# The output products of a feed-forward by seven block products in place of eight, with transferred low parts and moved conditioning rows

## The chip, the cores and the metric

The kernel runs on one core of a Trainium2 chip. The metric is the time of one execution on the device in microseconds, lower is better. The engines are TensorE (PE in the profile, its weight loads PEld), VectorE (DVE), ScalarE (ACT), GpSimd (POOL) and SyncE (SP, which issues most DMAs).

## The reference: what is computed

One decoder block on 512 tokens of width 1024, in fp32. Nine modulation vectors of 1024 come from the condition `c`; each of three sub-layers is normalised, scaled and shifted by them, and its result is added with a gate. The first and the last sub-layer are feed-forwards of hidden width 2816 (22 tiles of 128), at half weight:

```python
def swiglu(u, w_in, w_out):
    a, b = jnp.split(u @ w_in, 2, axis=-1)
    return (jax.nn.silu(a) * b) @ w_out
```

Between them stands the mixer: a pooling branch and a dilated attention with rotary queries and keys, both multiplied by sigmoid gates, summed and projected. A last RMSNorm gives the output.

## The kernel before

**High and low parts.** Every fp32 matrix product is made of three products of shorter numbers. An operand is split into a high part and a low part (what is left), and `mm3` or `product` sums high by high, high by low and low by high (lines 357 to 359; 739 to 741; 865 to 867). Weights come by DMA from HBM, 512 KB a chunk (128x1024), into raw buffers (SP's queue, line 235). ACT copies the high part into `whi` (line 312), DVE subtracts to get `wlo` (line 326). Both lie in a ring of seven chunks, and the splits run four products ahead of the one that TensorE works on (`look(4)`).

**Seven products for eight.** Where two hidden tiles of both halves are made together (`duo`), the product of 2x2 blocks is made by seven block products with sums before and behind (the scheme of Strassen and Winograd). A block product is 24 matmuls of 256 columns. The sums of activations come from `u_steps` (high copy at line 705, low part at 706; tiles `S0` to `S2`), the sums of weights from `make` on DVE (line 251, tiles X), and the results are put together by ACT copies out of the PSUM banks (line 746) and DVE adds. `out_quad` does the same for an output: four hidden tiles times eight output tiles, seven products, with its own sums of hidden tiles in `h_sums` (line 831 is ACT's copy, 828 the add). With `outer`, the low part of some of the seven weight chunks is made without DVE: ACT writes the negative high part into `wlo` (line 308), and an accumulating DMA of GpSimd's queue adds the weight from HBM (line 310).

**The feed-forwards.** `ffn` goes through five parts of hidden tiles, `PARTS` = (0..4, 4..8, 8..12, 12..16, 16..22). In each it makes the hidden tiles, with those of the next part's first duo, then multiplies the part by the output weights and adds to the state H. In the first feed-forward the tiles up to 7 are made singly (`ffn_pair`), the rest by duos, all low parts by DVE, and the outputs of all parts plainly: 96 matmuls of 512 columns for four parts (loop at line 970, H updated at line 985). In the second feed-forward the tiles up to 3 are single; the four first outputs go through `out_quad`, and two of every seven low parts (the fourth and the sixth chunk, counted from 0 numbers 3 and 5) come by transfer, in its duos from the second one on and in its block outputs.

**Conditioning rows.** The modulation vectors take 72 rows of 512 KB (`wada`), one DVE multiply with a running sum each (line 380). In the first feed-forward `bg()` does rows 24 to 47, beside the single tiles 6 and 7 and then one per output tile, from two buffers (`cs`, `AR`); the next row is fetched when a buffer is free. Rows 48 to 71 come in the mixer's end.

**The mixer.** It is written out in one order by hand; `mm_tile` takes hooks that run after a given block of a tile. Four value tiles (v23) precede the gates; `at_merge` (lines 1231 to 1248, DVE) combines the attention groups, `at_yT` transposes the result on TensorE (line 1255), and the low parts of the pooled branch (PL) stand at line 1290.

**Queues.** Each engine works its instructions in the order in which the program issues them; `later(n, f)` puts f behind the n-th product from now.

## Time and profile before

| | us |
|---|---|
| median of 3 runs | 1012.51 (1011.1 to 1012.77) |
| profiled execution | 1010.66 |
| its span | 1008.8 |
| plain output, parts 1 to 3 of the first feed-forward | 21.78 to 21.79 |
| block output, second feed-forward | 19.04 to 19.27 |

The granted clock of the profiled execution is 0.996 of full speed on average. A row of the timeline gives start, duration, engine, line, output and inputs, and in brackets how long the engine stood idle before it and what released it. A row of a group gives its count, its busy time and mean duration, then the idle time before it.

### The profile page before, as it was taken

The numbers are of one execution on the slowest core, as the hardware profiler recorded it, in microseconds if no ns is written. First come the engines' busy times: TensorE is split into PE (matmuls) and PEld (weight loads), VectorE is DVE, ScalarE is ACT, GpSimd is POOL, SyncE is SP. The second block draws the span as 40 slices with busy tenths as digits, with TensorE's granted clock in tenths as the row PEclk, the third lists the DMA queues.
The fourth block names the chain that finished last, engine by engine and source line by source line (L and its number), as shares of the span: only waits on it lengthen the run. The fifth ranks groups of instructions, "written<-read, shape, count | busy, mean of one in ns | idle before, by whom it ended". The sixth has DMA issues, their size and how long they took to land.

```text
span 1008.8 us, 16370 instructions
## 1 busy us (share of the span) xinstructions
PE 994.6 (99%) x6652; PEld 913.9 (91%) x6652; DVE 788.6 (78%) x1182; ACT 496.4 (49%) x754; POOL 47.3 (5%) x54
## 2 busy tenths in 40 slices
PE   8999999999999999999999999999899999999997
PEld 6888898989999999889988888898899999999996
DVE  7978879889787676879447777567998988989754
ACT  6443253625434552233414333463677768677652
POOL 0000000000000000007100000000011011011001
PEclk9999999999999999999999999999999999999998
DMA  9866456555533413122054774322467666756712
GB/s 341 275 224 228 140 195 189 175 164 185 168 99 117 145 46 99 58 84 84 32 185 161 272 261 134 92 78 63 146 147 178 177 147 155 201 130 164 178 32 84
DMA packets 46574, 152.24 MB, mean 151 GB/s; under 512 B 5281, under 2 KB 8609, under 8 KB 46498
## 3 DMA queue, kind: packets, MB, share of 16 engines
q1 hardware_dynamic: 42354, 137.95, 41.3%
q0 software_dynamic: 3456, 12.58, 7.5%
q8 instruction: 52, 0.85, 0.3%
q10 hardware_dynamic: 688, 0.66, 0.2%
q14 instruction: 24, 0.20, 0.1%
HBM read 148.40 MB, written 2.77 MB: 150 GB/s over the span
## 4 chain that ended last, share of the span: by engine, by line
PE 90%; DVE 7%; ACT 1%; issue 1%; DMA 0%; DVEq 0%; ACTq 0%
PE bank L357 14%; PE bank L358 14%; PE bank L359 14%; PE bank L739 10%; PE bank L741 9%; PE bank L740 9%; PE bank L867 3%; PE bank L866 3%; PE bank L865 3%; DVE wlo L326 1%; PE bank L1616 1%; PE bank L1620 1%; PE bank L1618 1%; PE bank L1212 1%; PE bank L1391 1%; PE bank L1392 1%
## 5 line engine op out<-in xcount | busy, mean ns | idle before, releaser
L326 DVE TENSOR_TENSOR wlo<-raw,whi 128x1024 fp32r<-128x1024 f32 (+7 forms) x157 | 156.7, 1011 | 56.0 <-ACT whi L312 55.8
L312 ACT ACTIVATE whi<-raw 128x1024 fp32r<-128x1024 f32 (+7 forms) x172 | 150.6, 894 | 31.2 <-DVE raw L251 27.6
L357 PE MATMUL bank<-UH,whi 128*128 128x512 f32 (+1 forms) x432 | 158.0, 366 | 0.0
L358 PE MATMUL bank<-UL,whi 128*128 128x512 f32 (+1 forms) x432 | 154.0, 357 | 0.1
L359 PE MATMUL bank<-UH,wlo 128*128 128x512 f32 (+1 forms) x432 | 153.9, 356 | 0.0
L741 PE MATMUL bank<-UH,wlo 128*128 128x256 f32 x512 | 141.6, 277 | 0.0
L739 PE MATMUL bank<-UH,whi 128*128 128x256 f32 x512 | 141.5, 276 | 0.0
L740 PE MATMUL bank<-UL,whi 128*128 128x256 f32 x512 | 141.5, 276 | 0.0
L326 DVE TENSOR_TENSOR wlo<-X,whi 128x1024 fp32r<-128x1024 f32 (+4 forms) x102 | 111.4, 1099 | 30.8 <-ACT whi L312 30.5
L312 ACT ACTIVATE whi<-X 128x1024 fp32r<-128x1024 f32 (+4 forms) x111 | 105.6, 966 | 40.6 <-DVE X L251 39.6
L739 PE MATMUL bank<-SH,whi 128*128 128x256 f32 x384 | 108.0, 281 | 3.0 <-ACT u L746 2.2
L740 PE MATMUL bank<-SL,whi 128*128 128x256 f32 x384 | 107.6, 280 | 0.0
L741 PE MATMUL bank<-SH,wlo 128*128 128x256 f32 x384 | 107.5, 280 | 0.0
L357 PE MATMUL bank<-HI,whi 128*128 128x512 f32 (+1 forms) x278 | 96.8, 348 | 0.0
L358 PE MATMUL bank<-HK,whi 128*128 128x512 f32 (+1 forms) x278 | 96.5, 347 | 0.0
L740 PEld LDWEIGHTS bank<-UL,whi 128*128 128x128 f32 x512 | 96.2, 188 | 0.2
L359 PE MATMUL bank<-HI,wlo 128*128 128x512 f32 (+1 forms) x278 | 96.4, 347 | 0.0
L741 PEld LDWEIGHTS bank<-UH,wlo 128*128 128x128 f32 x512 | 96.1, 188 | 0.2 <-DMA wlo<-wf2i 0.2
L739 PEld LDWEIGHTS bank<-UH,whi 128*128 128x128 f32 x512 | 96.1, 188 | 0.2
L359 PEld LDWEIGHTS bank<-UH,wlo 128*128 128x128 f32 x432 | 81.1, 188 | 12.1
L358 PEld LDWEIGHTS bank<-UL,whi 128*128 128x128 f32 x432 | 81.2, 188 | 11.7 <-issue 0.5
L357 PEld LDWEIGHTS bank<-UH,whi 128*128 128x128 f32 x432 | 81.2, 188 | 11.2 <-issue 0.5
(300 smaller groups left out, 2104.1 us busy)
## 6 DMA issues: line engine op xcount, KB each, us to landing
ada<-wada SPq DMA_DIRECT2D x47, 512.0 KB, 5.3
raw<-wmix SPq DMA_DIRECT2D x44, 512.0 KB, 4.1
raw<-wf1i SPq DMA_DIRECT2D x34, 512.0 KB, 4.5
raw<-wf2i SPq DMA_DIRECT2D x30, 512.0 KB, 3.7
wlo<-wf2i POOLq DMA_DIRECT2D x16, 512.0 KB, 6.3
X<-wf2i SPq DMA_DIRECT2D x14, 512.0 KB, 4.3
cs<-wada SPq DMA_DIRECT2D x12, 512.0 KB, 3.7
AR<-wada SPq DMA_DIRECT2D x12, 512.0 KB, 4.4
```

The lines of the kernel that those rows point to most:

```text
L312: self.nc.scalar.activation(self.hi[:, y], r[:, x], AF.Copy)
L326: self.nc.vector.tensor_tensor(self.lo[:, y], r[:, x], self.hi[:, y], op=OP.subtract)
L357: M(ps, hi, uh, start=start, stop=False)
L358: M(ps, hi, ul, start=False, stop=False)
L359: M(ps, lo, uh, start=False, stop=stop)
L739: M(o, hi, uh, start=start and p == 0 and k == 0, stop=False, skip_group_check=True)
L740: M(o, hi, ul, start=False, stop=False, skip_group_check=True)
L741: M(o, lo, uh, start=False, stop=k == 3, skip_group_check=True)
L865: M(o, hi, uh, start=start and m % 2 == 0 and k == 0, stop=False, skip_group_check=True)
L866: M(o, hi, ul, start=False, stop=False, skip_group_check=True)
L867: M(o, lo, uh, start=False, stop=k == 1, skip_group_check=True)
L1212: M(o, pt[:, blk * P:blk * P + P], v, start=i == 0, stop=i == len(srcs) - 1)
```

## The change

- The outputs of parts 1 to 3 (tiles 4 to 15) of the first feed-forward go through `out_quad`; its hidden sums and evictions come with it. Part 0 and the last part stay plain.
- In the first feed-forward's duos of tiles 10 to 21 and in its three block outputs, three of seven low parts (chunks 0, 3 and 5) come by transfer.
- The conditioning rows 24 to 39 are done in the first feed-forward, 24 to 27 with the single tiles 6 and 7, then two per duo (`beside`, after its third and sixth product). Rows 40 to 47 go to the mixer, into the one buffer `AR`, with one row fetched at a time.
- Buffers: the ring of hidden tiles has 4 places in the first feed-forward (`nh`), with three tiles `kept` of its own; the block outputs collect their results in `kept`; some high and low copies of hidden tiles come later (8 products behind a duo of the even kind, halves of tiles 4 and 5 after 5 and 6 products).
- Second feed-forward: `u_steps` puts a sum between each high copy and its low part, the low parts of tiles 0 to 3 are put off, and the hidden sums of part 0 start two products later.

Where it moves instructions (rows of the programs' order, without times; names with numbers are tiles). DVE in the mixer, around the start of the merge (`mm` is the merge's first operation, raw_66 and the like are weight buffers). Before:

```order
L326 TENSOR_TENSOR wlo<-raw_67,whi 128x1024
L1216 COPY q_3191<-bank_104 128x256
L326 TENSOR_TENSOR wlo<-raw_68,whi 128x512
L1290 SCALAR_TENSOR_TENSOR PL_3173<-bank_104,vecs,PH_3171 128x512
L1290 SCALAR_TENSOR_TENSOR PL_3174<-bank_98,vecs,PH_3172 128x512
L326 TENSOR_TENSOR wlo<-raw_66,whi 128x1024
L1231 TENSOR_TENSOR mm<-m_3200,v_3197 128x16
```

After:

```order
L1244 COPY q_3517<-bank_104 128x256
L381 SCALAR_TENSOR_TENSOR AR,mod<-AR,cond 128x1024
L327 TENSOR_TENSOR wlo<-raw_68,whi 128x512
L1318 SCALAR_TENSOR_TENSOR PL_3499<-bank_104,vecs,PH_3497 128x512
L1318 SCALAR_TENSOR_TENSOR PL_3500<-bank_102,vecs,PH_3498 128x512
L381 SCALAR_TENSOR_TENSOR AR,mod<-AR,cond 128x1024
L327 TENSOR_TENSOR wlo<-raw_66,whi 128x1024
L381 SCALAR_TENSOR_TENSOR AR,mod<-AR,cond 128x1024
L1259 TENSOR_TENSOR mm<-m_3526,v_3523 128x16
```

Three conditioning rows (44, 45 and 46, line 381 now) stand among the rows ahead of the merge, the last one directly before it.

DVE at the start of the second feed-forward (line 664, now 670, makes a hidden tile, 667 or 678 its low part HK; 699 or 725 are sums of activations, 706 or 733 the low part SL of one). Before:

```order
L664 TENSOR_TENSOR cond<-sl,bank_98 128x512
L667 TENSOR_TENSOR HK<-cond,HI 128x512
L715 TENSOR_TENSOR X<-UH,UL 128x1024 x2
L664 TENSOR_TENSOR cond<-p_5891,bank_100 128x512
L667 TENSOR_TENSOR HK<-cond,HI 128x512
L699 TENSOR_TENSOR X<-X 128x1024
L706 TENSOR_TENSOR SL_5609<-X,SH_5608 128x1024
L699 TENSOR_TENSOR X<-X 128x1024
```

After:

```order
L670 TENSOR_TENSOR cond<-sl,bank_98 128x512
L741 TENSOR_TENSOR X<-UH,UL 128x1024
L678 TENSOR_TENSOR HK<-cond,HI 128x512
L741 TENSOR_TENSOR X<-UH,UL 128x1024
L670 TENSOR_TENSOR cond<-u_6225,bank_100 128x512
L725 TENSOR_TENSOR X<-X 128x1024
L678 TENSOR_TENSOR HK<-cond,HI 128x512
L725 TENSOR_TENSOR X<-X 128x1024
L733 TENSOR_TENSOR SL_5951<-X,SH_5950 128x1024
```

Between a tile and its low part there now stands another sum.

ACT in the first feed-forward's output of part 1, from the first duo ahead of it (`sl` of the silu) on. Before:

```order
L769 ACTIVATE sl<-bank_97 128x2x256
L312 ACTIVATE whi<-X 128x256
L312 ACTIVATE whi<-X 128x768
L312 ACTIVATE whi<-X 128x1024
L746 ACTIVATE HI<-hf 128x1024
L312 ACTIVATE whi<-X 128x1024
L312 ACTIVATE whi<-raw_68 128x1024
```

After:

```order
L791 ACTIVATE sl<-bank_101 128x2x256
L313 ACTIVATE whi<-X 128x1024
L868 ACTIVATE bank_97<-bank_98 128x512
L868 ACTIVATE bank_102<-bank_99 128x512
L309 ACTIVATE wlo<-X 128x1024
L313 ACTIVATE whi<-X 128x1024
L868 ACTIVATE sl<-bank_100 128x512
L868 ACTIVATE sl<-bank_101 128x512
L313 ACTIVATE whi<-X 128x1024
L868 ACTIVATE kept_123<-bank_98 128x2x256
```

The copies out of the banks (line 868 now) and the negative copies for the transfers (line 309) stand among the high parts of the weights (line 313).

The diff, cut to its core:

```diff
-        def blocks(recs, outer=False):
+        def blocks(recs, outer=0):
             n = len(self.loads)
             if outer:
                 self.outer.update({len(self.order) + 3: n + 3, len(self.order) + 5: n + 2})
+            if outer == 3:
+                self.outer[len(self.order)] = n
...
                     else:
-                        blocks(ins[at:at + 4], n == 2 and j > PLAIN[n])
...
                         j, at = j + 2, at + 4
-                put = blocks if n and part < len(PARTS) - 1 else plain
+                put = blocks if (n or part) and part < len(PARTS) - 1 else plain
                 put(outs[part * KT // 2:(part + 1) * KT // 2] if part + 1 < len(PARTS) else outs[-KT:],
-                    **({"outer": True} if put is blocks else {}))
+                    **({"outer": (3, 0, 2)[n]} if put is blocks else {}))
...
+    def beside(self, j, i):
+        if self.nh == 4 and j > PLAIN[0] and i in (2, 5):
+            self.bg()
...
-    def ffn_post(self, j, s, pb):
+    def ffn_post(self, j, s, pb, between=None):
         nc = self.nc
-        h = self.kept[j // 2 % 3][:, j % 2 * T:j % 2 * T + T] if self.kept else self.fw.tile([P, T], F32, name=("hf", "u3")[j % 2])
+        h = self.kept[j // 2 % 3][:, j % 2 * T:j % 2 * T + T]
         nc.vector.tensor_tensor(h, s, pb, op=OP.mult)
-        hh, hl = self.HH[j % NH], self.HL[j % NH]
+        hh, hl = self.hh(j)
+        if self.nh == 4 and j in (4, 5):
+            t = slice(0, HT)
+            self.later(5, lambda: nc.scalar.activation(hh[:, t], h[:, t], AF.Copy))
+            self.later(6, lambda: nc.vector.tensor_tensor(hl[:, t], h[:, t], hh[:, t], op=OP.subtract))
+            return
         nc.scalar.activation(hh, h, AF.Copy)
-        nc.vector.tensor_tensor(hl, h, hh, op=OP.subtract)
+        low = lambda: nc.vector.tensor_tensor(hl, h, hh, op=OP.subtract)
+        if between is None:
+            return low()
+        between(low)
...
+        four = lambda i, u: u.rearrange("p (k t) -> p k t", k=4) if i == 3 else u
+        def high(i, u):
+            return lambda: nc.scalar.activation(self.S[i][0], four(i, u), AF.Copy)
+        def low(i, u):
+            return lambda: v.tensor_tensor(self.S[i][1], four(i, u), self.S[i][0], op=OP.subtract)
...
-        last = split(3, a12)
-        return ([whole(a11, 0), whole(a12, 4)] if n else []) + [add(a22, a21, a22, OP.add), split(0, a22), add(a21, a11, a21, OP.subtract), split(2, a21),
-                add(a11, a22, a11, OP.subtract), split(1, a11), add(a12, a12, a11, OP.subtract)], last
+        return ([whole(a11, 0), whole(a12, 4)] if n else []) + [
+            add(a22, a21, a22, OP.add), both(high(0, a22), add(a21, a11, a21, OP.subtract)),
+            both(high(2, a21), low(0, a22)), add(a11, a22, a11, OP.subtract), both(high(1, a11), low(2, a21)),
+            add(a12, a12, a11, OP.subtract), low(1, a11)], both(high(3, a12), low(3, a12))
...
-            self.later(2, high)
-            self.later(2, low)
+            n = 8 if self.nh == 4 and j % 4 == 0 else 2
+            self.later(n, high)
+            self.later(n, low)
...
+                self.later((2 if k0 else 4) + n, f)
...
-        D = [self.fw.tile([P, 2 * T], F32, name=n).rearrange("p (j h t) -> p j h t", j=2, h=2) for n in ("u2", "sl")]
-        p5 = [r(self.fw.tile([P, T], F32, name=n)) for n in ("p5", "p6")]
...
+        p5 = self.fw.tile([P, 2 * T], F32, name="sl")
+        p5 = [r(p5[:, i * T:(i + 1) * T]) for i in range(2)]
...
+            if self.nh == 4 and self.todo:
+                self.todo.pop(0)()
...
-        self.kept = [self.cond, self.cs, self.AR]
         bk = [self.nb() for _ in range(4)]
         self.head(2, bk, AF.Silu)
-        self.G = [(self.tp.tile([P, T], F32R, name="ut"), self.fw.tile([P, T], F32R, name=f"G{i}")) for i in range(3)]
+        self.open_G()
         self.todo, last = self.u_steps(2)
         do = lambda n: [self.todo.pop(0)() for _ in range(n)]
         for j in range(2):
-            self.ffn_post(j, self.ffn_silu(j, bk[2 * j]), bk[2 * j + 1])
-            do(2 + j)
+            self.ffn_post(j, self.ffn_silu(j, bk[2 * j]), bk[2 * j + 1], lambda low: (do(1), low(), do(1 + j)))
         pa = self.ffn_tile()
         do(len(self.todo))
-        self.ffn_post(2, self.ffn_silu(2, pa), self.ffn_tile())
-        self.ffn_pair(3)
+        due = []
+        self.ffn_post(2, self.ffn_silu(2, pa), self.ffn_tile(), due.append)
+        pa = self.ffn_tile()
+        due.pop()()
+        self.ffn_post(3, self.ffn_silu(3, pa), self.ffn_tile(), lambda low: self.later(1, low))
         self.ffn(2, 4, last)
...
         fp, self.fw, xp = (st.enter_context(self.tc.tile_pool(name=x, bufs=1)) for x in ("f", "fw", "fx"))
-        self.HHall, self.HLall = (fp.tile([P, NH * T], F32R, name=x) for x in ("HI", "HK"))
...
+        self.HHall, self.HLall = (fp.tile([P, nh * T], F32R, name=x) for x in ("HI", "HK"))
+        self.Gall = self.fw.tile([P, 3 * T], F32R, name="G")
+        self.kept = [self.fw.tile([P, 2 * T], F32, name=f"kept{i}") for i in range(3)] if nh == 4 else [self.cond, self.cs, self.AR]
...
             nk = k1 - k0
-            hk = [(self.HH[k % NH], self.HL[k % NH]) for k in range(k0, k1)]
...
+            hk = [self.hh(k) for k in range(k0, k1)]
+            if not tail and (n or part):
                 self.out_quad(k0, gate)
...
-                        if n == 0 and part:
-                            self.bg()
...
-            self.ada_free, self.ada_stop = [self.cs, self.AR], 48
+            self.ada_free, self.ada_stop = [self.cs, self.AR], 40
...
+            self.open_G()
...
+            self.ada_free, self.ada_stop, self.ada_depth = [self.AR], 48, 1
+            self.bg_fetch()
...
+                    if k == 6:
+                        self.bg()
...
             self.held = None
-            gates = [self.mm_tile(hooks([], [(4, self.at_swap)]))]
-            gates.append(self.mm_tile({2: [lambda: self.pool_map(0)], 4: [lambda: self.pool_map(1)]}))
...
-            gates.append(self.mm_tile())
...
             self.at_merge()
-            gates.append(self.mm_tile({7: [self.at_yT]}))
+            gates.append(self.mm_tile({4: [self.bg], 7: [self.at_yT]}))
...
-            self.ada_stop, self.ada_depth = 72, 4
+            assert self.ada_next == 48, self.ada_next
+            self.ada_free, self.ada_stop, self.ada_depth = None, 72, 4
...
-        with self.open_ffn():
+        with self.open_ffn(4):
...
-        with self.open_ffn() as self.f2:
+        with self.open_ffn(6) as self.f2:
```

More of the change, by code (lines that the diff above doesn't have):

```diff
@@ L73, in lay_ffn @@
     for k0, k1 in PARTS:
-        if blocks and k1 < FT:
+        if blocks <= k0 and k1 < FT:
             for i, c in ((0, 0), (0, 4), (1, 4), (1, 0)):
@@ L127 @@
 PARTS = ((0, 4), (4, 8), (8, 12), (12, 16), (16, 22))
-NH = 6
 def pairs_before(n, part):
@@ L787, in duo @@
             if i == 6:
-                v.tensor_tensor(q(c)[:, :, 1, :], p5, u3, op=OP.add)
-            self.look(3 if self.kept and first and i == 0 else 4)
+                v.tensor_tensor(c1, c1, u3, op=OP.add)
+            self.look(3 if self.nh != 4 and first and i == 0 else 4)
             self.product(bank, u, start)
@@ L959, in ffn @@
                 else:
-                    if self.kept and not tail and j == k1:
+                    if not tail and j == k1:
                         self.h_sums(k0)
```

79 lines of the change are left out of this document (39 added, 40 removed).

## The prediction

> **What bounds the kernel now.** I read the head of the page, then the chain that ended last, then the busy time of each engine in a stretch of the first feed-forward (140 to 320 us: three plain outputs and the duos between them) and of the second (740 to 920 us: three block outputs and duos). A row of stretches gives its length, the busy time of PE, PEld, DVE, ACT and POOL with the count of instructions, the granted clock, the DMA share and GB/s.
>
> ```profile
> span 1008.8 us, 16370 instructions
> PE 994.6 (99%) x6652; PEld 913.9 (91%) x6652; DVE 788.6 (78%) x1182; ACT 496.4 (49%) x754; POOL 47.3 (5%) x54
> PE 90%; DVE 7%; ACT 1%; issue 1%; DMA 0%; DVEq 0%; ACTq 0%
> 140.00:320.00 180.00, 179.95 (x1287) 168.46 (x1287) 153.31 (x187) 79.79 (x105) 0.00 (x0) 1.00 0.50 159
> 740.00:920.00 180.00, 180.00 (x1579) 179.73 (x1578) 160.09 (x195) 130.20 (x177) 15.67 (x18) 1.00 0.67 168
> ```
>
> TensorE is the bound nearly everywhere: it holds 90% of the chain, and in both stretches it has no gap. The time is the PE work, plus places where PE waits. So the change is worth what it takes off PE, less each new wait of PE. The second stretch shows what the first is to become, and that it runs without gaps at DVE 89%, ACT 72% and DMA 67%.
>
> **A. The converted outputs.** The three plain outputs of parts 1 to 3, then the four block outputs of the second feed-forward:
>
> ```profile
> 144.52:166.31 21.79, 21.79 (x99) 18.03 (x98) 18.23 (x25) 5.57 (x6) 0.00 (x0) 1.00 0.50 158
> 204.84:226.62 21.78, 21.78 (x98) 18.01 (x98) 19.14 (x32) 5.66 (x7) 0.00 (x0) 1.00 0.48 156
> 265.49:287.27 21.78, 21.78 (x98) 18.02 (x98) 19.02 (x27) 7.48 (x11) 0.00 (x0) 1.00 0.35 108
> 733.57:752.61 19.04, 19.04 (x170) 19.04 (x170) 17.26 (x22) 14.26 (x21) 2.26 (x3) 1.00 0.71 171
> 791.01:810.05 19.04, 19.04 (x170) 19.04 (x170) 17.31 (x23) 14.35 (x21) 2.25 (x3) 1.00 0.68 169
> 848.45:867.70 19.25, 19.25 (x170) 19.11 (x170) 17.53 (x23) 14.34 (x21) 2.30 (x3) 1.00 0.72 169
> 906.10:925.37 19.27, 19.27 (x170) 19.14 (x170) 17.65 (x23) 14.74 (x21) 2.32 (x3) 1.00 0.70 168
> ```
>
> 96 matmuls of 512 columns become 168 of 256: 21.78 becomes 19.04 us, 2.74 less. Three times: **-8.2 us**.
>
> **B. The start of the second feed-forward.** PE's wait there, the clock after it, ACT in front of it, and DVE's groups between 686 and 716 us with their idle time at the end:
>
> ```profile
> 700.00:740.00 40.00, 37.03 (x268) 35.07 (x267) 36.92 (x42) 26.26 (x37) 1.90 (x2) 0.96 0.42 128
> 715.71 0.38 PE L739 MATMUL bank<-SH,whi 128*128 128x256 f32 x1 [0.77 <-ACT bank L746]
> 723.63 0.58 PE L739 MATMUL bank<-SH,whi 128*128 128x256 f32 x1 [2.19 <-ACT u L746]
> 723.63:726.94 3.31, 3.31 (x16) 3.31 (x16) 3.31 (x4) 2.90 (x4) 0.00 (x0) 0.51 0.90 363
> 722.46 0.63 ACT L831 ACTIVATE ut<-cs 128x512 fp32r<-128x512 f32 x1 [0.68 <-DVE cs L828]
> 723.00 0.58 ACT L746 ACTIVATE u<-bank 128x512 f32<-128x512 f32 x1
> L706 DVE TENSOR_TENSOR SL<-X,SH 128x1024 fp32r<-128x1024 f32 x3 | 3.7, 1226 | 2.3 <-ACT SH L705 2.3
> L667 DVE TENSOR_TENSOR HK<-cond,HI 128x512 fp32r<-128x512 f32 x2 | 1.4, 693 | 1.4 <-ACT HI L666 1.4
> L667 DVE TENSOR_TENSOR HK<-cs,HI 128x512 fp32r<-128x512 f32 x2 | 1.4, 692 | 1.4 <-ACT HI L666 1.4
> ```
>
> PE loses 2.19 + 0.77 = 2.96 us, and after the longer wait the clock is 0.51 for 3.31 us, which costs 3.31 x 0.49 = 1.6 more; 4.6 in all. The 0.77 wait drops no clock. The cause stands in the ACT rows: the eviction `u` that frees PE's bank is queued behind a copy of the first sums (L831), which waits for DVE, and DVE is late because it stood idle 2.3 + 1.4 + 1.4 = 5.1 us, each time for the ACT copy whose low part it was to take next. The change puts another sum between copy and low part, and starts the sums of part 0 two products (5.4 us) later, so that the copy is no longer ahead of `u`. 5.1 us of DVE is more than the 2.96 that PE waits. What is late next may be the first block output's transfers, so I take **-4.0**, with 0.6 left; the ends are 0 (DVE only moves its holes) and -4.6.
>
> [...]
>
> **C. The gate rows in the mixer.** Eight rows leave the first feed-forward for one buffer, AR: the next transfer is issued only when the row before it is done. Most have time; the multiply of row 46, the last but one, stands on DVE ahead of the attention merge:
>
> ```profile
> AR<-wada SPq DMA_DIRECT2D x12, 512.0 KB, 4.4
> L380 DVE SCALAR_TENSOR_TENSOR AR<-AR,cond x12: 1215/1216/1224, 113.1 to 280.1; 128x1024 f32<-128x1024 f32 x12
> 513.18 0.38 SPq L1222 DMA_DIRECT2D v<-scr  x1
> 517.98 0.75 DVE L1290 SCALAR_TENSOR_TENSOR PL<-bank,vecs,PH 128x512 fp32r<-128x512 f32 x1 [1.50 <-ACT PH L1289]
> 520.07 0.17 DVE L1231 TENSOR_TENSOR mm<-m,v 128x16 f32<-128x16 f32 x1
> 525.94 0.42 DVE L1248 TENSOR_TENSOR o<-o,v 128x256 f32<-128x256 f32 x1
> 530.00 1.04 PE L1255 MATMUL bank<-cst,o 128*128 128x128 f32 x8
> ```
>
> Row 45 is fetched behind `v<-scr` (513.6) and lands at 518.0; its multiply follows the last PL (518.73) and ends at 519.95. Only then row 46 is issued; it lands 4.4 later at 524.4, is done at 525.6, and the merge behind it takes what it takes now, 520.07 to 526.36, 6.3 less a little overlap, 6.2: end 531.8. PE wants its transposes at 530.0: **+1.8**. What is queued behind is the merge and the split of the branch weights, for which PE's transposes and then the branch products wait. A landing 0.9 quicker or 1.1 slower gives 0.9 to 2.9.
>
> **D. Three transferred low parts per block in the first feed-forward.** Groups in 740 to 920 us, DMA queues of that stretch (packets, MB, share of 16 engines), landing of the accumulating transfers there (us, smallest, median, largest), and one block output's issues beside its first matmul:
>
> ```profile
> L326 DVE TENSOR_TENSOR wlo<-X,whi 128x1024 fp32r<-128x1024 f32 x32 | 39.1, 1222 | 9.0 <-ACT whi L312 8.9
> L308 ACT ACTIVATE wlo<-raw 128x1024 fp32r<-128x1024 f32 x10 | 10.5, 1051 | 0.0
> q1 hardware_dynamic: 5520, 20.08, 33.4%
> q0 software_dynamic: 2736, 9.96, 33.3%
> DMA to landing us min/median/max: 5.3/6.5/8.4
> 790.65 0.86 POOL L310 DMA_DIRECT2D wlo<-wf2o  x1 [13.33 <-ACT wlo L308]
> 790.84 0.28 PE L865 MATMUL bank<-HI,whi 128*128 128x256 f32 x1
> 796.30 0.88 POOL L310 DMA_DIRECT2D wlo<-wf2o  x1 [4.79 <-ACT wlo L308]
> ```
>
> Two duos and an output take 180 x 57.1 / 180 = 57.1 us of PE. In that cycle DVE now has 160.09 / 180 x 57.1 = 50.8 us in the second feed-forward. In the first it does three subtractions less (3 x 1.22) and four ada rows more (4 x 1.22): 52.0, 91%, and in one output the trig operations beside. ACT: 130.20 / 180 x 57.1 = 41.3, and 3 x 1.05 more is 44.5, 78%. Both stay under PE. DMA is closer. 20.08 MB of plain transfers are 38.3 of 512 KB, which took 0.334 x 180 / 38.3 = 1.57 us of all 16 engines each; 9.96 MB of accumulating ones are 19.0, at 0.333 x 180 / 19.0 = 3.15 us, twice as dear. The cycle's load is 0.67 x 57.1 = 38.3, and 3 x 3.15 + 4 x 1.57 more makes 54.0 of 57.1, 95%. It fits, barely. Chunk 5 is the one to watch: issued at 796.30 and needed five products (5 x 2.72) after 790.84, at 804.4, it has 8.1 us; the median is 6.5 and the largest 8.4. Two of the four block outputs are 0.2 longer than 19.04, which I read as such a late landing. Six duos and three outputs, nine blocks, at 0.2: **+1.9** (0 to 14, below).
>
> [...] In this stretch VectorE is busy 89% of the time:
>
> ```profile
> L310 POOL DMA_DIRECT2D wlo<-wf2i x12: 858/865/883, 750.5 to 891.6; - x12
> ```
>
> [...]
>
> **The sum**, against the profiled execution's 1010.66 (span 1008.8): 1010.66 - 8.2 - 4.0 + 1.8 + 1.9 = 1002.2. The median of the runs, 1012.51, lies 1.85 above that execution: **1004.0**. Everything else (other buffers, delayed copies of the hidden tiles, evictions into kept) lies on DVE and ACT beside PE and is in the loads of D; without that cover a copy would cost its 1.05 or 1.22.
>
> **Rivals**, all on the median's basis.
> - *Slower: the DMA engines are full in a duo with ada rows.* Such a duo moves four weight chunks and two rows, six times 1.57, and 3 x 3.15: 18.9 of its 19.0 us. If rows and accumulations collide, each block waits one more plain transfer: 9 x 1.57 = 14.1 in place of D's 1.9: **1016.2**. It decides once the landing rises from 6.5 by over 1.6 us. For it: the 95%; against it: 8.4 was the largest at 67%. Chance 0.12.
> - *The merge waits longer.* If row 46 lands in 6.5, as the accumulating transfers do, instead of 4.4, PE idles 3.9, and the clock falls as in B, 1.6 more: 5.5 instead of 1.8, **1007.7**. For it: three weight transfers go ahead of a row in SP's queue there. Chance 0.13.
> - *B gives nothing,* since the eviction's place on ACT, not DVE's holes, holds PE: **1008.0**. Chance 0.13.
> - *All is hidden:* no merge wait, no late landing, all of B: 1012.5 - 8.2 - 4.6 = **999.7**. Chance 0.13.
> [...]
>
> **How the numbers follow.** My forecast has 0.45. I take 999 to 1010.5 as the range: it holds all cases but the two dear ones (0.16) and the outer edges. A measurement of this kernel tells about 0.2% (2 us) from no change: faster is below 1010.5. The forecast and three rivals are faster, 0.84, less 0.02 for bad luck in two terms at once; the lock is the same, 0.06 with those; slower is the full-DMA case, 0.12.
>
> **What would show it.** A: three stretches of 19.0 us with 170 matmuls. B: no PE wait for `u` and clock 1.00 at the first duos of the second feed-forward. C: DVE waiting for AR ahead of `mm`, and PE for the transposes. D: PEld waiting for `wlo<-wf1i` and `wlo<-wf1o`, 0.2 a block; if it is over 1 us a block, my DMA sum is wrong. A PE wait for DVE or ACT inside a duo of parts 1 to 3 would make the claim wrong that their load fits.

## The result and the profile after

The changed kernel takes 1011.49 us in the median of 12 runs (1008.73 to 1015.41), the kernel before 1012.64 us in 12 runs beside it (1011.06 to 1014.56). The ratio is 0.9991 with a 95% interval from 0.9978 to 1.0005: no change that can be measured, where 1004.0 us was forecast and 1010.5 was the upper end. The profiled execution of the changed kernel took 1010.08 us.

The same views as before: the head, the chain, and the stretch of the first feed-forward with its block outputs.

```profile
span 1008.2 us, 16982 instructions
PE 992.4 (98%) x6868; PEld 921.4 (91%) x6868; DVE 800.7 (79%) x1224; ACT 546.3 (54%) x826; POOL 71.6 (7%) x81
PE 86%; DMA 5%; DVE 4%; issue 3%; ACT 1%; POOL 0%; DVEq 0%; POOLq 0%; ACTq 0%
140.00:320.00 180.00, 177.25 (x1540) 176.25 (x1539) 160.50 (x214) 134.93 (x185) 23.62 (x27) 1.00 0.86 222
```

PE still holds the chain, but DMA has come into it with 5%, and in 140 to 320 us PE is idle for 2.75 us where it had 0.05. The DMA share there rose from 0.50 to 0.86. So waits took the place of a part of the work that left PE. The first fence shows the three converted outputs and the first block output of the second feed-forward. The second shows PE's longest waits inside the two feed-forwards (line, total, times, longest). The third is the time from issue to landing of the accumulating transfers in 120 to 330 us (smallest, median, largest):

```profile
149.61:169.00 19.39, 19.39 (x170) 19.31 (x169) 16.68 (x22) 15.01 (x21) 3.48 (x4) 1.00 0.85 198
208.21:228.30 20.09, 19.41 (x170) 19.21 (x169) 17.56 (x30) 14.78 (x21) 3.41 (x4) 1.00 0.89 220
266.70:286.43 19.73, 19.32 (x170) 19.12 (x169) 18.02 (x27) 15.37 (x24) 3.42 (x4) 1.00 0.91 224
731.33:751.70 20.37, 19.69 (x170) 19.48 (x169) 19.45 (x27) 16.01 (x24) 2.64 (x3) 1.00 0.59 155
```

```profile
PE bank L766 <- ACT kept L773: 1.2, 1, 1.2
PE bank L888 <- DMA wlo<-wf1o: 1.1, 2, 0.7
PE bank L888 <- DMA wlo<-wf2o: 0.7, 1, 0.7
PE bank L768 <- DMA wlo<-wf1i: 0.4, 1, 0.4
```

```profile
DMA to landing us min/median/max: 5.4/7.5/9.5
```

The converted outputs hold 168 matmuls as forecast (the rows count neighbours at their ends with them), but last 19.4 to 20.1 us instead of 19.0. Each wait in the list is either for a low part by transfer (`wlo`) or for the bank's eviction in the first duo.

**Where the time went.** The span can be cut on PE's timeline, from the first matmul of a stretch to the first of the next. "First feed-forward" runs from its first duo to the end of its last one, "second" from its first duo to the end of its last one; the middle holds the plain output of the last part and the mixer. What lies between the start and the first duo takes 65.28 us in every profile and is left out. The third kernel is the changed one with two conditioning rows moved in the mixer only (run e3 below): up to there, and in the second feed-forward, its code is the changed kernel's.

| us | before | after | e3 |
|---|---|---|---|
| start, from PE's first matmul to the first product of tile 4 | 56.48 | 60.15 | 57.58 |
| first feed-forward, duos and outputs | 200.61 | 196.57 | 199.96 |
| last plain output and mixer | 383.43 | 386.74 | 385.08 |
| second feed-forward, duos and outputs | 254.83 | 251.26 | 253.07 |

Two things stand in this table. The first feed-forward gains 4.0 and 0.6 us in two executions of one and the same code, not the 8.2 - 1.9 = 6.3 forecast; how long PE waits for transferred low parts differs from one execution to the next (1.1 + 0.4 us in 120 to 330 us in the changed kernel's, 2.2 + 1.2 in e3's). And the start alone, where PE's work is the same in all kernels, differs by 3.7 us. Here are the last matmuls of the norm's sums, before and after:

```profile
14.17 1.50 PE L1545 MATMUL bank<-H,ones 128*128 128x128 f32 x12
```

```profile
17.37 2.63 PE L1578 MATMUL bank<-H,ones 128*128 128x128 f32 x12
```

The same twelve matmuls take 1.50 and 2.63 us: after, PE worked there at 0.57 of the pace of before. Over the fourteen profiles of this study the start takes 56.5 to 60.2 us. It takes 59.89 in e4, whose start is the code of before, and 56.8 to 57.1 in six that have the changed kernel's, so the change isn't the cause. The profiled execution of before had the shortest start of all. That may be a part of why it lies 2 us under its own median, but it isn't shown: the changed kernel's profiled execution has a long start, 60.15, and lies 1.4 us under its own.

Taken without the start, the change moved its profiled execution by -4.3 us; without it and with e3's two feed-forwards, it would be some +1. One profile doesn't tell, so here is the same cut over all profiles with the same code in a stretch. The first feed-forward of the changed kernel stands in two: -2.3 us against before on the mean. Its second feed-forward stands in eleven (the changed kernel's and all variants but e4 and e11), at 250.9 to 254.9 us: -1.8 on the mean. Its middle, with the rows 46 and 47 around the merge, stands in six, at 386.0 to 387.0: +3.0. The sum is -1.1, and the medians moved by -1.15. That the two agree so closely with so few profiles is luck in part, but it says where the 8.5 us of the forecast went: 4.0 short in the first feed-forward, 2.2 in the second, 1.2 in the middle.

### The profile page after: what moved, and what is told of

It is laid out like the page before. It is cut to its first block, busy times and chain, and to the rows that moved or that the text cites. A ratio compares the mean times of both kernels' runs of the same rounds, so it can differ in the third digit from the quotient of the medians.

```text
span 1008.2 us, 16982 instructions
## 1 busy us (share of the span) xinstructions
PE 992.4 (98%) x6868; PEld 921.4 (91%) x6868; DVE 800.7 (79%) x1224; ACT 546.3 (54%) x826; POOL 71.6 (7%) x81
## 4 chain that ended last, share of the span: by engine, by line
PE 86%; DMA 5%; DVE 4%; issue 3%; ACT 1%; POOL 0%; DVEq 0%; POOLq 0%; ACTq 0%
PE bank L358 12%; PE bank L359 12%; PE bank L360 12%; PE bank L768 9%; PE bank L766 9%; PE bank L767 9%; PE bank L888 3%; PE bank L886 3%; PE bank L887 3%; DMA wlo<-wf1i 2%; DMA wlo<-wf1o 2%; PE bank L1649 1%; PE bank L1651 1%; PE bank L1653 1%; PE bank L1240 1%
## 5 line engine op out<-in xcount | busy, mean ns | idle before, releaser
L327 DVE TENSOR_TENSOR wlo<-raw,whi 128x1024 fp32r<-128x1024 f32 (+5 forms) x126 | 136.0, 1089 | 53.9 <-ACT whi L313 53.7
L313 ACT ACTIVATE whi<-raw 128x1024 fp32r<-128x1024 f32 (+5 forms) x157 | 149.0, 961 | 30.5 <-DVE raw L252 19.5
L313 ACT ACTIVATE whi<-X 128x1024 fp32r<-128x1024 f32 (+3 forms) x135 | 116.8, 886 | 30.3 <-DVE X L252 30.2
L327 DVE TENSOR_TENSOR wlo<-X,whi 128x1024 fp32r<-128x1024 f32 (+3 forms) x115 | 109.3, 971 | 28.1 <-ACT whi L313 27.7
L766 PEld LDWEIGHTS bank<-SH,whi 128*128 128x128 f32 x384 | 72.4, 189 | 1.5 <-ACT kept L773 1.4
L767 PEld LDWEIGHTS bank<-SL,whi 128*128 128x128 f32 x384 | 72.4, 189 | 0.0
L768 PEld LDWEIGHTS bank<-SH,wlo 128*128 128x128 f32 x384 | 72.4, 189 | 0.0
```

What stands on the lines that cost most here:

```text
L313: self.nc.scalar.activation(self.hi[:, y], r[:, x], AF.Copy)
L327: self.nc.vector.tensor_tensor(self.lo[:, y], r[:, x], self.hi[:, y], op=OP.subtract)
L766: M(o, hi, uh, start=start and p == 0 and k == 0, stop=False, skip_group_check=True)
L767: M(o, hi, ul, start=False, stop=False, skip_group_check=True)
L768: M(o, lo, uh, start=False, stop=k == 3, skip_group_check=True)
```

## The experiments

Ratios are against the kernel before, from runs beside it on the same chip, with their 95% interval. "The output of part 2" is the second converted one. Lengths are read as in the table above.

**e1: the first output's sums later.** In the first duo PE waited for `kept`, and ScalarE's rows show why (after):

```profile
140.16 0.63 ACT L851 ACTIVATE ut<-kept 128x512 fp32r<-128x512 f32 x1 [1.34 <-DVE kept L848]
140.70 0.58 ACT L773 ACTIVATE kept<-bank 128x512 f32<-128x512 f32 x1
```

It is the pattern of term B, moved to the first feed-forward: a copy of the new hidden sums (`ut`) waits 1.34 us for VectorE, and the eviction that PE needs stands behind it. The change delays these sums where `k0` is 0, and the first converted output has `k0` 4.

```diff
-                self.later((2 if k0 else 4) + n, f)
+                self.later((2 if k0 > 4 or (k0 and self.nh != 4) else 4) + n, f)
```

> The changed kernel with the hidden sums of its first converted output (tiles 4 to 7) two products later, as the change did in the second feed-forward. Theory (each loss of the profile is a wait of its own): the 1.4 us that PE waits in the first duo for the copy out of its bank, queued on ScalarE behind a copy that waits for VectorE, goes; that duo takes 19.4 instead of 20.9 us, and nothing else changes. Rival (VectorE and ScalarE are full there, so that a wait taken away comes back in the block output behind it): duo and output together stay at 40.3 us. On the start: if its 60.2 us up to the first block of 512-column matmuls come from the change, every kernel built on the changed one shows them; if they come from the moment at which the clock rises, some show 56.5.

Measured: 1012.16 us, ratio 0.9997 (0.9982 to 1.0013). The duo and the output behind it:

```profile
125.81:145.25 19.44, 19.44 (x169) 19.38 (x168) 17.16 (x20) 15.36 (x22) 1.28 (x2) 1.00 0.66 198
145.25:165.94 20.69, 19.62 (x171) 19.22 (x169) 18.70 (x26) 15.90 (x23) 3.20 (x4) 1.00 0.82 198
```

The duo falls from 20.93 to 19.44 as the theory says, and the output grows from 19.39 to 20.69, its first low part now late: 40.1 together against 40.3. The rival holds. The wait for the bank is real, but behind it stands the next one.

**e2: two transferred low parts instead of three in the first feed-forward.**

```diff
-                        blocks(ins[at:at + 4], (3, 0, 2)[n] if j > PLAIN[n] else 0)
+                        blocks(ins[at:at + 4], 2 if j > PLAIN[n] else 0)
...
-                    **({"outer": (3, 0, 2)[n]} if put is blocks else {}))
+                    **({"outer": 2} if put is blocks else {}))
```

> The changed kernel with two instead of three transferred low parts per block in the first feed-forward (chunks 3 and 5; chunk 0 by VectorE again). Theory of late transfers: the DMA load of two duos and an output falls from 54 to 44.5 of 57 us, the waits for wlo (some 2 us in the three outputs, 1 in the duos) go, so 2 to 3 us less than the changed kernel. Rival: VectorE, 52.0 plus 3 x 1.22 = 55.7 of 57.1 us, becomes the bound, and PE waits for its low parts or evictions instead; then the same or slower by some us.

Measured: 1016.64 us, ratio 1.0026 (1.0011 to 1.0042). Its waits of PE in 124 to 326 us and the stretch:

```profile
PE bank L888 <- DMA wlo<-wf1o: 3.6, 3, 1.5
PE bank L768 <- DMA wlo<-wf1i: 1.7, 1, 1.7
```

```profile
140.00:320.00 180.00, 173.94 (x1505) 172.65 (x1505) 165.94 (x217) 123.57 (x171) 15.79 (x18) 1.00 0.72 186
```

The rival holds again, and in a telling way: with a DMA share of 0.72 instead of 0.86 PE waits *more* for transferred low parts, 5.3 us against 1.5. Full DMA engines alone cannot be the cause. What is late is the issue of the transfer: in the three outputs chunk 5 is issued 6.7, 7.9 and 7.7 us after the first matmul (5.5 to 6.8 in the changed kernel), with VectorE 92% busy.

**e3: the merge freed.** Rows 46 and 47 go to the end of the mixer's gates.

```diff
-            gates.append(self.mm_tile({4: [self.bg]}))
+            gates.append(self.mm_tile())
             self.at_merge()
-            gates.append(self.mm_tile({4: [self.bg], 7: [self.at_yT]}))
+            gates.append(self.mm_tile({7: [self.at_yT]}))
```

> The changed kernel with the conditioning rows 46 and 47 done at the end of the mixer's gates instead of around the attention merge. Theory: the merge starts at once after its operands, PE no longer waits for the sums of the groups before its transposes; 0.7 to 1.0 us less in the mixer. Rival: the merge is not on PE's path, and the wait shows elsewhere: no change in the mixer's length. The 1.3 us gap of PE's weight loads at the start of the mixer's last product, which nothing in the profile releases, stays if it belongs to the code's place, and goes if it is a chance of that execution.

Measured: 1011.54 us, ratio 0.999 (0.9977 to 1.0004). Last plain output and mixer take 385.08 instead of 386.74: 1.7 less, at a ratio that can't be told from the changed kernel's. Over all profiles the stretch takes 384.8 to 386.1 us with this edit (six) and 386.0 to 387.0 without (six), so the edit is worth some 1.2 on the mean. VectorE and PE in the changed kernel around the merge, then the gap near the mixer's end (weight load, matmul, and the VectorE row that the matmul's bracket names), and last the VectorE row of the same place before the change:

```profile
524.16 1.22 DVE L381 SCALAR_TENSOR_TENSOR AR<-AR,cond 128x1024 f32<-128x1024 f32 x1 [0.31 <-DMA AR<-wada]
525.31 0.17 DVE L1259 TENSOR_TENSOR mm<-m,v 128x16 f32<-128x16 f32 x1
531.66 0.77 PE L1283 MATMUL bank<-cst,o 128*128 128x128 f32 x5 [0.52 <-DVE o L1276]
```

```profile
648.62 0.19 PEld L358 LDWEIGHTS bank<-MH,whi 128*128 128x128 f32 x1 [1.33 <-issue]
648.65 0.36 PE L358 MATMUL bank<-MH,whi 128*128 128x256 f32 x1 [0.94 <-DVE H L1493]
647.75 0.75 DVE L1493 SCALAR_TENSOR_TENSOR H<-bank,mod,H 128x512 f32<-128x512 f32 x1 [1.81 <-PE bank L360]
```

```profile
646.05 0.75 DVE L1460 SCALAR_TENSOR_TENSOR H<-bank,mod,H 128x512 f32<-128x512 f32 x1 [1.81 <-PE bank L359]
```

The row, the merge behind it and PE's wait stand where they were forecast, with the merge from 525.3. PE's transposes waited 0.5 only, since the first three need just the first groups; the extra time from them to the branch products is 0.7 us. e3 has no such wait. The gap before the first matmul of the mixer's last product is another matter: it costs PE 1.10 us at that very matmul in the changed kernel, is there in each of its eleven variants here, and is not there in the kernel before nor in e4. So it belongs to the program, not to chance. The weight load's bracket says only "issue", but the matmul's names VectorE's update of H for the tile before. That update ends at 648.50, and PE starts 0.15 us later. Before the change the same update runs from 646.05 to 646.80 beside PE's matmuls of the last product, which begin at 645.85 without a wait. The update reads a bank, the matmul writes one, and the two share nothing else, so the product seems to begin now in the bank that VectorE still reads. Why the banks fall so was not tried.

**e4: the reorder alone.** The kernel before with the second feed-forward's new start (`u_steps`, `ffn_post` with `between`, `h_sums` later for `k0` 0), and nothing else.

> The kernel before with only the reordered sums at the start of the second feed-forward (sums between high copy and low part, low parts put off, first hidden sums two products later). Theory: 3.5 to 4.5 us faster than before, all of it in the first duo (24.3 to 19.4 us), less up to 1.3 us in the first block output, whose transferred low parts are late. Rival: the gain there comes from the changed kernel's other moves (its tiles and buffers), and the reorder alone gives under 1 us.

Measured: 1009.67 us, ratio 0.9967 (0.995 to 0.9983). First duo and first block output of the second feed-forward:

```profile
712.66:731.99 19.33, 19.33 (x169) 19.32 (x168) 18.29 (x21) 14.39 (x19) 0.51 (x1) 1.00 0.47 164
731.99:751.32 19.33, 19.33 (x171) 19.13 (x169) 18.42 (x24) 15.25 (x23) 2.24 (x3) 1.00 0.66 164
```

The duo falls from 24.34 to 19.33, the output grows by 0.3 only, and the second feed-forward by this gains 4.6 us in the profiles; by the ratio the kernel gains 3.3, just under the 3.5 to 4.5 of the theory. By the medians this one part of the change gives more than the whole change, though the intervals touch (up to 0.9983 here, from 0.9978 there). In the changed kernel the same output takes 20.37, and in its eleven variants 20.4 to 22.4.

**e5 and e6: the rows in the duos, taken out whole, and as transfers only.** In e5 a small memset stands for a row's multiply, and nothing is fetched; in e6 the multiply stays, on what the buffer holds.

```diff
         if self.nh == 4 and j > PLAIN[0] and i in (2, 5):
-            self.bg()
+            n = self.ada_next
+            self.nc.vector.memset(self.mod[:, n:n + 1], 0.0)
```

> The changed kernel without the conditioning rows 28 to 39 that stand in the first feed-forward's duos: neither transferred nor multiplied (their sums are set to zero, so the mixer's scale and shift are not the reference's). Theory (the late low parts of the block outputs come from the rows): the three block outputs, 19.4 to 21.0 us in the profiles so far, fall to 19.1 to 19.4, the duos behind them to 38.4 to 38.6, 3 to 6 us less than the changed kernel. Rival (three transferred low parts per block are too many by themselves): the outputs stay above 19.8 us each and the time falls by under 2 us.

> The changed kernel with the rows 28 to 39 multiplied but not transferred (VectorE multiplies what the two buffers hold, so these sums are not the reference's). Theory V (the row's multiply stands on VectorE ahead of the weight sum that ScalarE and then the transfer of chunk 5 wait for, 1.3 us each time): the block outputs stay as long as in the changed kernel, 19.4 to 21.0 us, and chunk 5 is issued 6.8 us after the output's first matmul as now. Theory D (the rows' transfers lengthen the landing of the accumulating ones, 7.5 to 7.9 us instead of 6.5): the outputs fall to 19.1 to 19.4 us and the median landing to 7.0 or less.

Measured: e5 1007.82 us, ratio 0.9956 (0.9943 to 0.9969); e6 1012.06 us, ratio 0.9988 (0.9973 to 1.0004). The outputs of parts 1 to 3, first e5, then e6:

```profile
146.58:165.66 19.08, 19.08 (x171) 19.08 (x169) 16.37 (x22) 15.01 (x21) 3.49 (x4) 1.00 0.86 198
205.17:224.21 19.04, 19.04 (x171) 19.04 (x170) 15.92 (x25) 14.62 (x20) 2.62 (x3) 1.00 0.87 199
263.12:282.16 19.04, 19.04 (x171) 19.04 (x169) 15.52 (x23) 15.31 (x23) 2.62 (x3) 1.00 0.90 205
```

```profile
146.80:165.84 19.04, 19.04 (x170) 19.04 (x169) 16.33 (x22) 15.01 (x21) 3.50 (x4) 1.00 0.88 198
204.81:225.73 20.92, 19.33 (x171) 19.13 (x169) 18.71 (x31) 14.88 (x21) 3.42 (x4) 1.00 0.80 187
264.54:284.22 19.68, 19.33 (x171) 19.13 (x170) 17.98 (x27) 15.36 (x24) 3.42 (x4) 1.00 0.79 191
```

Both kernels leave out what the mixer needs of these rows, so they serve for the time alone. Without the rows all three outputs are 19.0 to 19.1. With the multiplies but without their transfers, parts 2 and 3 are long again, at a *lower* DMA share. Theory V holds: it is the multiply. Its path in the changed kernel's output of part 2, whose first matmul starts at 208.21 (VectorE, ScalarE, GpSimd, PE):

```profile
208.37 1.22 DVE L381 SCALAR_TENSOR_TENSOR AR<-AR,cond 128x1024 f32<-128x1024 f32 x1
...
210.32 1.22 DVE L252 TENSOR_TENSOR raw<-raw,raw 128x1024 f32<-128x1024 f32 x1
```

```profile
211.57 1.06 ACT L313 ACTIVATE whi<-raw 128x1024 fp32r<-128x1024 f32 x1 [2.41 <-DVE raw L252]
...
213.53 1.05 ACT L309 ACTIVATE wlo<-raw 128x1024 fp32r<-128x1024 f32 x1
```

```profile
214.98 0.88 POOL L311 DMA_DIRECT2D wlo<-wf1o  x1 [5.98 <-ACT wlo L309]
```

```profile
222.97 0.39 PE L888 MATMUL bank<-HI,wlo 128*128 128x256 f32 x1 [0.68 <-DMA wlo<-wf1o]
```

The row's multiply stands ahead of the weight sum (`raw`); ScalarE waits 2.41 us for the sum, its negative copy for chunk 5 comes after that, GpSimd issues the transfer 6.8 us after the output's first matmul, and PE, which comes to the low part of chunk 5 13.9 us after it (at 222.1), waits. In e5 the same rows are:

```profile
205.01 1.22 DVE L252 TENSOR_TENSOR raw<-raw,raw 128x1024 f32<-128x1024 f32 x1
```

```profile
208.58 1.06 ACT L309 ACTIVATE wlo<-raw 128x1024 fp32r<-128x1024 f32 x1
```

```profile
210.04 0.88 POOL L311 DMA_DIRECT2D wlo<-wf1o  x1 [5.21 <-ACT wlo L309]
```

The transfer is issued 4.9 us after the first matmul (205.17), 1.9 us earlier, and nothing waits. What e5 leaves in the duos (two of them are 1.0 and 0.4 us longer, with waits for `wlo<-wf1i`) is chunk 0, which needs no row to be late.

**e7: rows moved into the outputs** of parts 2 and 3, from the duos ahead of them.

```diff
-        if self.nh == 4 and j > PLAIN[0] and i in (2, 5):
+        if self.nh == 4 and j > PLAIN[0] and j not in (12, 16) and i in (2, 5):
             self.bg()
...
+            if self.nh == 4 and k0 > 4 and i in (2, 4):
+                self.bg()
```

> The changed kernel with the two rows of each duo that stands ahead of a block output (tiles 12, 13 and 16, 17) moved into the block outputs of parts 2 and 3, behind their third and fifth product, where VectorE has idle time of its own. Theory V: chunk 5 of the outputs of parts 2 and 3 is issued 5.6 instead of 6.8 us after the first matmul, these two outputs fall by 0.8 to 1.3 us each, 1.5 to 2.5 us in all. Theory D (landing time): the outputs get rows of their own to transfer, and stay or grow.

Measured: 1011.38 us, ratio 0.9984 (0.9969 to 0.9999). Chunk 5 of these outputs is issued as early as in e5, and part 2 takes 19.04, part 3 19.65. But the duos between and behind the outputs take 118.7 us together instead of 116.4: their chunk 0 is late instead, and the median landing of all transfers rises from 7.5 to 8.4 us. Half of the expectation: the place was right, the load came out elsewhere.

**e8: e1, e3 and e7 together.**

> The changed kernel with three edits: the rows moved as in the run that moves them into the block outputs, the first output's hidden sums two products later, and the rows 46 and 47 behind the merge. If the waits are separate: 1.5 to 2.5 for the rows, 0.2 to 1.4 for the sums, 0.7 to 1.0 for the merge, 2.5 to 4.5 us less than the changed kernel. If the first feed-forward's transfers hold PE anyway: only the merge's 1 us.

Measured: 1009.08 us, ratio 0.9975 (0.9962 to 0.9988). By the ratios 1.6 us below the changed kernel, under the 2.5 that separate waits would give at the least. Its outputs of parts 2 and 3 take 19.55 and 19.04 and the mixer falls as in e3, but the last duos take 39.9 and the second feed-forward's first output 22.35: there, too, a part comes back as late low parts (PE waits 2.50 us for one in that output).

**e9: rows early.** The rows of the duos ahead of an output go beside the single tiles 6 and 7 (two each time instead of one), with e3's edit. **e10:** the same with two transferred low parts. **e11:** e10, with the second feed-forward's first sums one product later instead of two.

```diff
                 self.bg()
-                if part == 0:
+                if part <= 1:
                     self.bg()
```

> The changed kernel with no conditioning row in the duos ahead of a block output (tiles 12, 13 and 16, 17): four more rows go beside the single tiles 6 and 7, where the DMA engines have idle time; and the rows 46 and 47 behind the merge. Theory V (multiplies ahead of chunk 5) gives the outputs of parts 2 and 3 at 19.0 to 19.4 us, as without rows, and leaves 0.4 to 0.9 us in most duos, whose chunk 0 is issued when the ring has room and lands after 7.5 us or more: some 4.5 us below the kernel before. If the rows' number and not their place decides, the outputs stay at 19.7 and above.

> The same with two instead of three transferred low parts per block in the first feed-forward. If VectorE is the bound with two (the run of two low parts alone was 4 us slower than the kernel before), it stays slower than the run with three, since 52.0 - 2.4 + 3.7 = 53.3 of 57.1 us are left on VectorE, with chunk 5 issued late again. If only the rows ahead of a block output did that, the first feed-forward becomes like the second: outputs 19.0 to 19.3, duos 38.4 to 38.6, some 6 us below the kernel before.

> The run with two transferred low parts and the rows early, with the first hidden sums of the second feed-forward one product later than before the change instead of two. The first block output there takes 20.4 to 22.4 us in the changed kernel and its variants, its chunk 5 issued 7.2 us after the output's first matmul. If the two products' delay puts VectorE behind there, it is issued a product's share earlier and the output falls to 19.0 to 19.6 us, 1 us or more; against it stands that the copy may block the bank's eviction again: then PE waits in the first duo, which grows from 19.3 by 1 us or more.

Measured: e9 1009.63 us, ratio 0.9974 (0.9957 to 0.9991); e10 1009.2 us, ratio 0.9964 (0.9949 to 0.998); e11 1011.11 us, ratio 0.998 (0.9966 to 0.9994). The outputs of parts 2 and 3 in e9:

```profile
209.73:228.77 19.04, 19.04 (x170) 19.04 (x169) 15.71 (x25) 14.62 (x20) 2.62 (x3) 1.00 0.81 199
267.18:286.22 19.04, 19.04 (x171) 19.04 (x170) 15.49 (x23) 15.31 (x23) 2.61 (x3) 1.00 0.92 206
```

At a DMA share up to 0.92 they run without a wait, so in the outputs place decides, not load. In e10 two duos together fall to 38.4 to 38.7 as well, as forecast for a first feed-forward like the second. But the times miss what was expected: by the ratios 2.6 us below the kernel before instead of 4.5 (e9), and 3.6 instead of 6 (e10). One reason is the first duo. With four more rows ahead of it, it is 22.0 (e9) and 23.5 us (e10) long: ScalarE's eviction comes later still, and in e10 the clock falls after the wait. The wait, and the stretch behind it:

```profile
133.62 0.38 PE L766 MATMUL bank<-SH,whi 128*128 128x256 f32 x1 [2.26 <-ACT bank L773]
133.62:137.20 3.58, 3.58 (x18) 3.58 (x19) 2.73 (x4) 2.58 (x4) 0.00 (x0) 0.56 0.53 151
```

e11 misses: the first block output of the second feed-forward stays at 20.9 us, and the duo ahead of it at 19.33. The number of products by which the sums are put off is not what makes that output long.

**e12: e8 with two transferred low parts.**

> The run of all three edits (rows of the duos ahead of a block output moved into the outputs, first hidden sums later, merge free) with two instead of three transferred low parts in the first feed-forward. If a multiply ahead of chunk 5 and a chunk 0 that lands too late are the two losses there, both are gone: outputs of parts 2 and 3 19.0 to 19.7, duos 38.4 to 38.7, the first duo 19.4, from the first duo to the end of the last one some 194 us against 200.6 before, and the kernel 5 to 7 us below the one before. Rival: VectorE with two low parts is too full when rows stand in the outputs (55.7 of 57.1 us, as in the run of two low parts alone); then no faster than the run of all three edits, 0.9975 of the kernel before.

Measured: 1011.95 us, ratio 0.9996 (0.9982 to 1.001). The rival holds. The outputs of parts 2 and 3 take 19.04 both, as expected, but the first output takes 21.4 and two of the duos 22.2 and 20.8. Its stretch, to be set beside e2's:

```profile
140.00:320.00 180.00, 174.47 (x1514) 173.07 (x1513) 168.86 (x222) 125.95 (x173) 15.79 (x18) 1.00 0.73 191
```

VectorE is 94% busy, and PE waits both for low parts and for evictions (4.0 and 1.5 us in 124 to 326 us).

No version beats e4 clearly (e5 leaves work out). e4, e10, e9 and e8 lie at 0.9964 to 0.9975 with intervals that overlap; e4 is the one with the least in it.

## Why the prediction was wrong

**A, the matmuls: right.** 168 matmuls in 19.04 us per output, seen undisturbed in e5 and e9. All of the 8.2 us is there to be had.

**D, three transferred low parts: the step that failed.** It put 0.2 us on each of nine blocks, 1.9 in all. Beside the first duo, the first feed-forward is 2.6 us (the changed kernel's profile) and 6.0 us (e3's) longer than A alone would make it. The loads were not the fault: VectorE 89% and DMA 86% in 140 to 320 us, where the prediction had 91% and 95%. The mechanism was: what decides is when one transfer is issued and when it lands, and both were read wrongly.

The issue time of chunk 5 was taken from the second feed-forward, where no conditioning row stands on VectorE. e5 and e6 show that the multiply of a row pushes it back by 1.9 us, through the weight sum and ScalarE's queue. And the landing was read as a median of 6.5 us over two kinds of transfer. In the second feed-forward before the change the outputs' chunk 3 lands after 5.3 to 5.9 us, but chunk 5 after 7.6, 8.2, 8.4 and 8.4. Here is chunk 5 of the output at 790.84 before, then that of the output at 208.21 after:

```profile
L310 POOL DMA_DIRECT2D wlo<-wf2o x1: 883/883/883, 796.3 to 796.3; - x1
DMA to landing us min/median/max: 8.2/8.2/8.2
```

```profile
L311 POOL DMA_DIRECT2D wlo<-wf1o x1: 881/881/881, 215.0 to 215.0; - x1
DMA to landing us min/median/max: 7.9/7.9/7.9
```

So of the 8.1 us from issue to need nothing was left over in three of the four outputs before the change, where the median let the prediction see 1.6. A later issue shows at once. In the changed kernel's output of part 2 it comes 6.8 us after the first matmul instead of 5.5, the landing takes no longer, and the output is 1.05 us over 19.04. In the outputs, then, it is the row's place and not the DMA share that decides; e2 and e9 say the same. In the duos chunk 0 is late, in e5 too: it is issued some 8.7 us ahead of the duo, and where PE waits for it, it lands after 9.2 to 10.1 us. In e10 chunk 0 has no transfer, and the duos fall; that doesn't tell whether the DMA load makes it late.

**The first duo: left out.** It grew by 1.6 us. Term B told exactly this mechanism (an eviction queued behind a copy that waits for VectorE) for the second feed-forward. The change brings `h_sums` into the first one, for a duo where VectorE is late too (the copy `ut` waits 1.34 us for it), and the prediction put that work under "beside PE". By e1 the 1.6 would not have been saved by moving the sums alone: the output behind the duo lost most of it.

**B, -4.0: right by the duo, -5.0, but half lost behind it.** The first block output gives 1.3 us of it back in the changed kernel's profile, where 0.6 was set aside, and the second feed-forward gains 3.6. That execution is one of the best. Over the eleven profiles with this code the output gives back 1.3 to 3.3, and the second feed-forward gains 1.8 on the mean; in the longest of them (254.9 us against 254.83 before) nothing is left of the gain. e4, with the reorder alone, gains 4.6 there in its one profile, and its time falls by 0.33%. Why the output is longer in the changed kernel than in e4 stays open. A low part that e4 makes 24.5 us ahead of the first duo is made 11.7 us ahead in the changed kernel, so VectorE starts one operation later and chunk 5 is issued 7.2 instead of 6.2 us after the first matmul. What put the low part there wasn't tried.

**C, +1.8: right in its place, too large for the merge, too small for the stretch.** The merge began as forecast, but cost 1.0 with what follows it, since PE's first three transposes need only the first groups. The last output and the mixer grew by 3.3 in all: 1.1 is the wait for VectorE's update near the end, which the prediction has nothing about, and the rest comes in small pieces, most of them ahead of the merge.

**The rivals.** The first one had the sign and a part of it: transfers that land too late in every block, 1016.2. Its condition (landing over 8.1 us in a full duo) is met in part: median 7.5, largest 9.5. It lacked the row's multiply. No run shows the lock that the chances name. What the runs show in its place: GpSimd's issues in the changed kernel's first feed-forward take 862 to 997 ns, where the row of before has 858 to 883 in the second, and one of 0.86 us, begun at 208.14, has the row's multiply of 208.37 beside it. The merge didn't wait longer, B did not give nothing, and not all was hidden.

**The basis.** The sum was made against an execution whose start was the shortest of all seen, 56.48 us of 56.5 to 60.2, and carried over to the median by adding 1.85. That is right on average, but it hides that up to 3.7 us of chance lie in a single profile, almost half of the gain that was to be seen.

## What to carry to other kernels

Work that is moved beside a busy engine must be placed by its queue, and not by its load alone. Here the output of part 3 takes 19.73 us at a DMA share of 0.91 in the changed kernel and 19.04 at 0.92 in e9, with the rows placed elsewhere. So ask for every moved instruction which later one, on any engine, waits in order behind it, and what deadline that one has. Count a transfer's lead time from its issue, and follow the issue back through the engines that prepare it: in the output of part 2 chunk 5 is issued 6.8 us after the first matmul with a row's multiply of 1.22 us ahead of the weight sum, 4.9 us without it (e5), and in the changed kernel it lands 7.9 us after its issue. And a profile compared with one other profile should be cut into stretches first; what neither edit touches shows how much of the difference is chance (here up to 3.7 us, in the start alone).

## What the runs showed of the hardware

PE's pace at the start differs from one execution to the next with the same instructions: the start takes 56.5 to 57.6 us in ten profiles and 59.9 to 60.2 in four. The granted clock reads 1.00 over it in twelve, the four long ones among them; in e3 and e12 it reads 0.50 for 3.41 us of it.

Inside the kernel, idle times of PE of 2.19 us (before), 2.26 us (e10) and 2.28 us (e11) were followed by some 3.5 us at a clock of 0.51 to 0.56, and one of 1.20 us (the changed kernel's first duo) by none. But a longer wait, of 2.50 us in e8 (its first block output of the second feed-forward), was followed by none either:

```profile
742.97 0.39 PE L888 MATMUL bank<-HI,wlo 128*128 128x256 f32 x1 [2.50 <-DMA wlo<-wf2o]
742.97:746.47 3.50, 3.50 (x30) 3.50 (x31) 3.50 (x6) 3.01 (x4) 0.86 (x1) 1.00 0.12 47
```

So in these runs the length of a wait alone doesn't tell whether the clock falls after it.
